# A streaming encoder step on one core: the first norm's additions and three weight splits move from GpSimd to VectorE, and the last 256 tokens of the final projection change layout

## The chip, the cores and the metric

The kernel runs on one core of one Trainium2 chip. A core has five engines that run side by side: TensorE (PE: matrix products from SBUF into the accumulation memory PSUM; the loading of its stationary operand is shown apart as PEld), VectorE (DVE), ScalarE (ACT), GpSimd (POOL) and SyncE (SP), which here only issues transfers. The metric is the device time of one execution in microseconds (us), the median over runs; lower is better. A single profiled execution supplies all durations.

## What is computed

One inference step of a two-layer encoder for 1024 frames of a new stream and 32 frames of a running one (1056 tokens, 1024 channels, fp32). The first layer has a pooling mixer, a gated MLP over chunks and a gate; the second is latent attention with a gate. Every layer normalises its input and its output:

```python
h = rms_norm(x, g_pre)                       # layer input
z = jnp.einsum('btd,de->bte', h, w_in)
...                                          # mixers, gate
y = jnp.einsum('bte,ed->btd', mix, w_out)
x = x + rms_norm(y, g_post)                  # residual
```

with `rms_norm(x, g) = x * rsqrt(mean(x*x, over channels) + 1e-6) * g`. The last lines of the second layer are `y = (o * silu(gate)) @ w_o` and `x + rms_norm(y, norm_post[1])`, where `w_o` is 1024 x 1024. The two places that matter here are the sum of squares of the very first norm and this last projection with its norm.

## The kernel before

All activations lie with channels on the 128 partitions and tokens along the free dimension, as eight blocks of 128 channels (index `k` or `m`). The tokens are cut into group a (640 tokens) and group b (416), in the last projection into 800 and 256. To keep fp32 accuracy, each operand of a product is split into two fp32r parts, hi (a rounded copy, written by ACT) and lo (the value less hi), and a product is three matmuls: hi x hi, hi x lo, lo x hi.

**Weights.** `prep_w` (L133 to L146) brings a weight block in pieces of 512 columns: SP loads a `raw` tile (three slots), ACT casts it to `whi` (L143), and an engine subtracts to get `wlo` (L144): GpSimd, unless the call passes `lo_on=nc.vector`. `whi` and `wlo` have four slots each in the common pool `stg`; calls with `pool=` get slots in a pool of their own (six each).

**Order.** TensorE's order is the order of the program text. The other engines' orders are set by a scheduling planner that simulates the kernel when it is built. Side jobs are generators: `spawn` gives one a due time in modelled TensorE nanoseconds (table `N`), and `poll`, called in the matmul loops, steps the one that is due; `drain` runs what is left. Their matmuls thereby get fixed places in TensorE's order.

**The head** (`even`, L301 to L370). Weight blocks 8 and 9 of `w1` and the eight channel blocks of x are loaded. For group a and then b, and for each `k`, `split_x` writes hi (ACT, L323) and lo (DVE, L324) of x times the pre-norm gain, TensorE multiplies with blocks 8 and 9, and `sumsq` squares x (ACT, L278 and L281) and adds the square to an accumulator (L282): on GpSimd for group a, on VectorE for group b. The norm itself is applied later, to the products: `rstd` (L193 to L233) sums the accumulator over the partitions on TensorE (L202), takes the power -1/2 on GpSimd (L210), and spreads the result over the partitions by diagonal matrices (L220), matmuls and copies (L233) into `rep`. `evac` (L185, L187) multiplies the products by `rep`, and with that frees the PSUM banks for block 10, prepared at L359, whose matmuls follow.

**The tail** (`output`, L1020 to L1098, and `final_a`, L1100 to L1118). The gated attention output comes back from DRAM by `load_og` and is split. Then the projection runs over the 800 tokens for output blocks `m` = 0 to 7, with weights `w[m]`; each result is copied (L1047), squared (L1052) and accumulated (L1053). `final_a`, spawned after that, makes the norm of these tokens and writes the output: per block a fused product on DVE (L1113), the residual addition (L1114) and a store. While it runs, TensorE does the 256 tokens, blocks 7 down to 0, where blocks 7 to 3 still lie in SBUF (3 to 5 in the six slots of pool `wx`) and 2 to 0 are loaded again. ACT squares each result and applies the gain (L1076, L1077), DVE accumulates (L1079). At the end come the column sums (L1068), the power on GpSimd (L1088), the spreading by diagonals (L1092, L1093) and, in quarters, product, residual and store (L1096 to L1098).

Of the kernel before, what the change touches and what calls it, by code (L numbers as in the profile page):

```python
# [10 lines left out]
F32 = mybir.dt.float32  # L11
F32R = mybir.dt.float32r
AF = mybir.ActivationFunctionType
ALU = mybir.AluOpType
# [5 lines left out]
P = 128  # L20
D = 1024
NK = 8
T = 1056
NA, NB, CA = 640, 416, 320
OA = 400
# [8 lines left out]

N = {"x": 462, "mix": 10626, "mixq": 1490, "tr": 717, "lead": 9945, "tr0": 11989, "res": 9194, "ra": 2699,
     "rb": 1574, "ha": 14000, "hb": 5000, "kv": 429, "q": 20908, "k": 34682, "kvs": 1773, "qs": 10662, "rest": 1357, "r1": 1608,
     "r2": 1337, "fa": 5400, "st": 6975, "w0": 2000, "w1": 1552, "f0": 1645, "f1": 626, "fy": 648}
HF = 6
RB = 4
LU = 5  # L40
NV = 1184
EPS = 1e-6
WARM = 12
# [3 lines left out]
GA1, GP1, GA2, GP2, PSC, LNG, LNB, QN, KVN = 0, 8, 16, 24, 32, 40, 48, 56, 59  # L47
# [23 lines left out]
class Build:  # L71
# [61 lines left out]
    def prep_w(self, src, n=1024, lo_on=None, pool=None):  # L133

        nc = self.nc
        res = []
        for o in range(0, n, 512):
            m = min(512, n - o)
            raw = self.t(self.stg, [P, 512], F32, "raw", bufs=3)
            hi = self.t(pool or self.stg, [P, 512], F32R, "whi", bufs=6 if pool else 4)  # L140
            lo = self.t(pool or self.stg, [P, 512], F32R, "wlo", bufs=6 if pool else 4)
            nc.sync.dma_start(raw[:, :m], src[:, o : o + m])
            nc.scalar.copy(hi[:, :m], raw[:, :m])  # L143
            (lo_on or nc.gpsimd).tensor_tensor(lo[:, :m], raw[:, :m], hi[:, :m], ALU.subtract)  # L144
            res.append((hi, lo))
        return res  # L146
# [138 lines left out]
    def even(self):  # L285
        nc = self.nc
# [9 lines left out]
        wts = {8: [], 9: []}  # L296
# [3 lines left out]
            nc.tensor.matmul(warm, self.ones, self.ones[:, None, :].to_broadcast([P, 4, P]), start=True, stop=True)  # L300
        for half in range(2):  # L301
            for i in range(2):
                wts[8 + i] += self.prep_w(self.i_w1[8 + i, :, half * 512 : half * 512 + 512], 512)
                if half == i == 0:
                    nc.sync.dma_start(xs[0][:, :NA], self.i_xT[0, :, :NA])
            for k in range(half * 4 + (half == 0), half * 4 + 4):
                nc.sync.dma_start(xs[k][:, :NA], self.i_xT[k, :, :NA])
# [4 lines left out]
        rep = self.new_rep()  # L312
# [35 lines left out]
        for g in "ab":  # L348
            acc = self.t(self.ab2, [P, NA if g == "a" else NB], F32, g)
            z = [None, None]  # L350
            for k in range(NK):
                x = split_x(g, k)
                for i in range(2):
                    z[i] = self.mm_block(self.wcol(wts[8 + i]), h, [k], g, ps=z[i], first=k == 0, last=k == 7)
                self.sumsq(acc, x, k == 0, g, nc.gpsimd if g == "a" else nc.vector, self.ab2)
            self.spawn(self.rstd(acc, g, D, rep.get(g)), N["x"])
            if g == "a":
                zz = z
        wts[10] = self.prep_w(self.i_w1[10])  # L359
        self.pos = 2  # L360
        mB[2] = self.pair(self.ab2)
        for g, z in (("a", zz), ("b", z)):
# [40 lines left out]
        for q in range(4):  # L403
            for j in range(2):
                nc.tensor.matmul(rss[:, q * 32 : (q + 1) * 32], self.ones[:32, :], wsp[q // 2][:32, q % 2, j, :32],
                                 start=j == 0, stop=j == 1)
        Cs = self.t(evc, [P, NK, 32], F32, "Cs")
        for m in range(NK):
            q = m // 2
# [163 lines left out]
        for i in range(8):  # L573
# [8 lines left out]
            if i >= 1:  # L582
                m = i - 1
# [9 lines left out]
        y = [None] * NK  # L593
        self.h2 = h2 = [None] * NK
        self.rep2 = self.new_rep()
        for g in "ab":
            n = NA if g == "a" else NB
            acc = self.t(self.V, [P, 1088], F32, "v")[:, :n] if g == "a" else self.t(self.ab2, [P, n], F32, "a")
            order = list(range(NK)) if g == "a" else list(reversed(range(NK)))
            for m, nm in zip(order, order[1:] + [None]):  # L600
# [10 lines left out]
                src = ps[0][:, :, :CA] if g == "a" else ps[1][:, :NB]  # L611
                v = two if g == "a" else (lambda z: z)
# [162 lines left out]
    def attention(self):  # L775
# [178 lines left out]
        for x, (h, i) in enumerate(steps):  # L954
# [17 lines left out]
            units(0.75)  # L972
            if h == 7 and i == LU:
                self.shut(self.carry)
                self.hl = self.open("hl", side="right", bufs=2 * HF)
                self.og = {}
            if h == 7 and i >= LU:
                for k in range(2 * (i - LU), min(HF, 2 * (i - LU + 1))):
# [41 lines left out]
    def output(self, w2, z2):  # L1020
        nc = self.nc
        na, nb = 2 * self.ca, self.nb
        hl = self.open("hlb")
        tp = self.open("tp", bufs=3)
        yp = self.open("yp", bufs=8)
        wx = self.open("wx")
        ones = self.t(tp, [P, P], F32, "ones", bufs=1)
        nc.gpsimd.memset(ones, 1.0)
        og = self.og
        w = dict(enumerate(w2))  # L1030
        for k in range(HF, 8):
            self.load_og(k, "a", hl, tp)
        for k in range(NK):
            self.load_og(k, "b", hl, tp)

        acc = self.t(tp, [P, na], F32, "acca", bufs=1)
        y = []
        for m in range(NK):
            if m in (0, 2, 3, 4, 5, 6):
                n = max(2, m + 1)  # L1040
                w[n] = self.prep_w(self.i_wo[n], pool=wx if 3 <= n < 6 else None)
            if m < 2:
                ps = self.mm_block(self.wcol(w[m]), og, range(HF, 8), "a", ps=z2[m], first=False)
            else:
                ps = self.mm_block(self.wcol(w[m]), og, range(NK), "a")
            yy = self.t(yp, [P, na], F32, "a")
            nc.vector.tensor_copy(two(yy), ps[0][:, :, : na // 2])  # L1047
            if m == 0:
                nc.scalar.activation(acc, yy, AF.Square)
            else:  # L1050
                sq = self.t(tp, [P, na], F32, "a", bufs=2)
                nc.scalar.activation(sq, yy, AF.Square)  # L1052
                nc.vector.tensor_tensor(acc, acc, sq, ALU.add)  # L1053
            y.append(yy)
        self.spawn(self.final_a(acc, y, tp, yp, na), N["fa"])


        acc = self.t(tp, [P, nb], F32, "accb", bufs=1)
        y = self.t(yp, [P, NK, nb], F32, "yb", bufs=1)
        x = self.t(yp, [P, NK, nb], F32, "xb", bufs=1)  # L1060
        nc.sync.dma_start(x, self.x1d[:, :, na:].rearrange("m p n -> p m n"))
        st = []

        def stats(src, first):
            for j in range(nb // P):
                if first:
                    st.append(self.bank("mi"))
                nc.tensor.matmul(st[j][:, 0:1], src[:, j * P : (j + 1) * P], self.one, start=first, stop=not first)  # L1068
            yield 0

        for m in reversed(range(NK)):
            if 3 <= m < 6:
                w[m - 3] = self.prep_w(self.i_wo[m - 3], lo_on=nc.vector)
            z = self.mm_block(self.wcol(w[m]), og, range(NK), "b")[1][:, :nb]
            sq = acc if m == 7 else self.t(tp, [P, nb], F32, "b")
            nc.scalar.activation(sq, z, AF.Square)  # L1076
            nc.scalar.activation(y[:, m], z, AF.Copy, scale=self.vec(GP2, m))  # L1077
            if 0 < m < 7:
                nc.vector.tensor_tensor(acc, acc, sq, ALU.add)  # L1079
            if m == 1:  # L1080
                self.spawn(stats(acc, True), N["st"])
        self.drain()
        for _ in stats(sq, False):
            pass
        ms = self.t(self.cst, [P, 8], F32, "sm", bufs=4)[:, : nb // P]
        for j in range(nb // P):
            nc.vector.tensor_scalar(ms[:, j : j + 1], st[j][:, 0:1], 1.0 / D, EPS, ALU.mult, ALU.add)
        nc.gpsimd.tensor_tensor(ms, ms, self.mhalf[:, : nb // P], ALU.pow)  # L1088
        rep = self.bank("za")[:, 0, :nb]
        for j in range(nb // P):  # L1090
            dg = self.t(tp, [P, P], F32, "dg", bufs=2)
            nc.vector.tensor_scalar(dg, self.ident, ms[:, j : j + 1], None, ALU.mult)  # L1092
            nc.tensor.matmul(rep[:, j * P : (j + 1) * P], ones, dg, start=True, stop=True)  # L1093
        for q in range(4):
            v = slice(2 * q, 2 * q + 2)
            nc.vector.tensor_tensor(y[:, v], y[:, v], rep[:, None, :].to_broadcast([P, 2, nb]), ALU.mult)  # L1096
            nc.vector.tensor_tensor(y[:, v], y[:, v], x[:, v], ALU.add)
            (nc.sync if q % 2 else nc.scalar).dma_start(self.o_yT[v, :, na:].rearrange("m p n -> p m n"), y[:, v])  # L1098

    def final_a(self, acc, y, tp, yp, n):  # L1100
        nc = self.nc
# [38 lines left out]
def pack(x_prompt, x_sample, cache_pool, cache_ckv, cache_krope, norm_pre, norm_post, w_in_even, w_pool, pool_scale,  # L1140
         sgu_ln_g, sgu_ln_b, w_spatial, b_spatial, w_out_even, w_in_odd, q_norm, kv_norm, w_q_up, w_kv_up, w_o):
    c = np.ascontiguousarray
    a = {}
# [26 lines left out]
    a["wo"] = c(w_o[0].reshape(NK, P, NK, P).transpose(2, 1, 0, 3).reshape(NK, P, 1024))  # L1170
    cc = cache_ckv[0, 0].T.reshape(2, P, P).transpose(1, 0, 2)
    ck = np.concatenate([cache_krope[0, 0].T] * 2, 0)[:, None]
    a["cache"] = c(np.concatenate([cc, ck], 1))
    pos = np.concatenate([np.arange(1024), 128 + np.arange(32)]).astype(np.float32)
    freqs = np.float32(10000.0) ** (-np.arange(32, dtype=np.float32) / np.float32(32))
# [5 lines left out]
    return a  # L1181


OUTS = {"yT": (NK, P, T), "st": (P, NK, 30), "sv": (32, D), "ckvT": (2, P, T), "krT": (64, T)}


@with_exitstack
# [26 lines left out]
```

## Time and profile before

| | us |
|---|---|
| median of 3 runs | 1336.59 (1332.97 to 1336.67) |
| the profiled execution | 1338.32 |
| its span, first to last instruction | 1336.5 |
| busy in the span: PE, DVE, ACT, POOL | 1297.6, 706.2, 491.2, 406.1 |
| mean granted TensorE clock | 0.986 |

The profile's times count from the start of the span. A row in order of time gives start, duration, engine, line of the kernel, operation, output and inputs, shape and count, and in brackets how long the engine had been idle and what released it. A group's row gives busy time and mean duration in ns, then idle time and its releasers. A row by stretch gives the stretch, its length, the busy time and instruction count of PE, PEld, DVE, ACT and POOL, the granted clock, the share of the DMA engines that is busy, and GB/s.

### The profile page before, as it was taken

Reading aid. Unit: us, or ns where it says so; the run is one execution under the profiler, and the core shown is the slowest. Engines: PE = TensorE matmul, PEld = TensorE weight load, DVE = VectorE, ACT = ScalarE, POOL = GpSimd, SP = SyncE. Lnnn points to the kernel's source line nnn. Section 1 sums busy time; section 2 is a strip of 40 time slices with the busy share of each in tenths; the row PEclk is TensorE's granted clock in tenths of the full one; section 3 lists DMA queues with packets and bytes.
Section 4 is the critical chain, followed back from the end, with each engine's and each line's share of the span. In section 5 each row is a group of like instructions: output and inputs, shape, how many; then the busy total and the mean of one; then the engine's idle time right before and its main releaser. Section 6 shows DMA issues by size and latency. Waiting matters only on the chain.

```text
span 1336.5 us, 21136 instructions
## 1 busy us (share of the span) xinstructions
PE 1297.6 (97%) x8244; PEld 1269.4 (95%) x8244; DVE 706.2 (53%) x1359; ACT 491.2 (37%) x968; POOL 406.1 (30%) x452
## 2 busy tenths in 40 slices
PE   8899999999999999999999989999999999999995
PEld 7899999999999999999999989999999999998994
DVE  7412021976956443533286642743666666665337
ACT  6212122222123333422154322434556565645221
POOL 6322112577743222200001354322223322323200
PEclk9899999999999999999999989999999999999997
DMA  5111111111111111222266333322111111126305
GB/s 191 48 48 56 48 40 48 40 40 33 52 43 45 52 48 40 70 73 78 63 215 194 109 111 102 119 83 65 46 49 46 47 46 51 47 65 219 97 25 179
DMA packets 63155, 102.62 MB, mean 77 GB/s; under 512 B 9232, under 2 KB 28080, under 8 KB 63056
## 3 DMA queue, kind: packets, MB, share of 16 engines
q1 hardware_dynamic: 51168, 86.17, 21.3%
q10 hardware_dynamic: 11888, 15.11, 3.2%
q8 instruction: 65, 1.06, 0.3%
q14 instruction: 34, 0.28, 0.1%
HBM read 82.34 MB, written 18.91 MB: 76 GB/s over the span
## 4 chain that ended last, share of the span: by engine, by line
PE 84%; DVE 7%; issue 3%; ACT 1%; DMA 1%; POOL 1%; ACTq 0%; DVEq 0%; POOLq 0%
PE za L108 36%; PE zb L108 21%; PE pj L108 12%; PE sc L108 11%; PE pj L905 2%; PE mi L108 1%; DMA raw<-in_wout 1%; PE mi L202 1%; PE mi L423 1%; ACT sw L829 0%; DVE b L324 0%; DVE b L637 0%; DVE b L659 0%; DVE v L536 0%; DVE b L648 0%
## 5 line engine op out<-in xcount | busy, mean ns | idle before, releaser
L108 PE MATMUL za<-a,whi 128*128 128x320 f32 x2112 | 463.6, 314 | 1.9 <-ACT a L323 1.2
L108 PEld LDWEIGHTS za<-a,whi 128*128 128x128 f32 x2112 | 371.8, 189 | 5.2 <-ACT a L323 1.6
L144 POOL TENSOR_TENSOR wlo<-raw,whi 128x512 fp32r<-128x512 f32 (+2 forms) x168 | 223.1, 1331 | 418.8 <-ACT whi L143 398.9
L108 PE MATMUL zb<-b,whi 128*128 128x416 f32 x1024 | 339.1, 356 | 1.5 <-DVE b L187 1.5
L143 ACT CAST whi<-raw 128x512 fp32r<-128x512 f32 (+2 forms) x230 | 139.3, 607 | 515.9 <-PE zb L108 260.8
L108 PE MATMUL za<-a,wlo 128*128 128x320 f32 x1056 | 242.0, 311 | 1.9 <-POOL wlo L144 1.8
L108 PEld LDWEIGHTS zb<-b,whi 128*128 128x128 f32 x1024 | 194.0, 191 | 2.5 <-DVE b L187 1.6
L108 PEld LDWEIGHTS za<-a,wlo 128*128 128x128 f32 x1056 | 192.1, 189 | 3.0 <-POOL wlo L144 2.5
L108 PE MATMUL zb<-b,wlo 128*128 128x416 f32 x512 | 181.2, 354 | 0.7 <-DVE wlo L144 0.7
L185 DVE TENSOR_TENSOR a<-za,repa 128x640 f32<-128x640 f32 x38 | 31.1, 821 | 162.9 <-PE za L108 162.8
L878 POOL TENSOR_SCALAR p<-p,nm 128x128 f32<-128x128 f32 (+8 forms) x72 | 53.0, 736 | 164.3 <-DVE nm L877 129.0
L108 PEld LDWEIGHTS zb<-b,wlo 128*128 128x128 f32 x512 | 98.1, 192 | 1.6 <-DVE wlo L144 1.0
L210 POOL TENSOR_TENSOR sm<-sm,mhalf 32x1 f32<-32x1 f32 (+3 forms) x17 | 15.3, 906 | 237.9 <-DVE sm L209 237.9
L144 DVE TENSOR_TENSOR wlo<-raw,whi 128x512 fp32r<-128x512 f32 x62 | 42.3, 688 | 56.8 <-ACT whi L143 56.8
L876 ACT ACTIVATE p<-sc,nm 128x128 f32<-128x128 f32 (+8 forms) x72 | 50.6, 703 | 44.7 <-DVE nm L875 33.3
L108 PE MATMUL sc<-a,whi 128*128 128x400 f32 x256 | 57.7, 346 | 0.7 <-DVE a L1047 0.4
L908 DVE TENSOR_TENSOR pl<-pj,ph 128x512 fp32r<-128x512 f32 (+2 forms) x96 | 51.1, 552 | 7.0 <-ACT ph L907 6.3
L875 DVE TENSOR_REDUCE nm<-sc 128x1 f32<-128x128 f32 (+8 forms) x72 | 50.7, 704 | 3.2
L907 ACT CAST ph<-pj 128x512 fp32r<-128x512 f32 (+2 forms) x96 | 43.8, 481 | 20.4 <-PE pj L905 18.1
L108 PEld LDWEIGHTS sc<-a,whi 128*128 128x128 f32 x256 | 46.3, 188 | 1.6 <-DVE a L1047 0.7
L108 PE MATMUL pj<-pl,vh 128*128 128x256 f32 (+1 forms) x160 | 45.1, 282 | 0.2 <-DVE pl L908 0.2
L108 PE MATMUL pj<-ph,vl 128*128 128x256 f32 (+1 forms) x160 | 45.0, 281 | 0.0
(292 smaller groups left out, 2300.7 us busy)
## 6 DMA issues: line engine op xcount, KB each, us to landing
raw<-in_w SPq DMA_DIRECT2D x120, 256.0 KB, 2.7
raw<-in_wout SPq DMA_DIRECT2D x60, 256.0 KB, 3.1
raw<-in_wo SPq DMA_DIRECT2D x22, 256.0 KB, 3.1
gt<-gated SPq DMA_DIRECT2D x32, 128.0 KB, 2.5
ogd<-og ACTq DMA_DIRECT2D x32, 128.0 KB, 2.6
v<-in_xT SPq DMA_DIRECT2D x16, 208.0 KB, 4.5
rawa<-x1d SPq DMA_DIRECT2D x8, 400.0 KB, 3.9
out_yT<-a SPq DMA_DIRECT2D x8, 400.0 KB, 4.6
```

The lines of the kernel that those rows point to most:

```text
L108: self.nc.tensor.matmul(out, lhsT, rhs, start=start, stop=stop)
L143: nc.scalar.copy(hi[:, :m], raw[:, :m])
L144: (lo_on or nc.gpsimd).tensor_tensor(lo[:, :m], raw[:, :m], hi[:, :m], ALU.subtract)
L185: nc.vector.tensor_tensor(two(dst.a), ps[0][:, :, :CA], two(rep.a), ALU.mult)
L202: nc.tensor.matmul(st[:w, j : j + 1], acc[:, j * P : j * P + w], self.one, start=True, stop=True)
L210: nc.gpsimd.tensor_tensor(m[:w, c0:c1], m[:w, c0:c1], self.mhalf[:w, c0:c1], ALU.pow)
L875: nc.vector.tensor_reduce(nm[:n, 0:1], view, axis=AX.XY, op=ALU.max, negate=True)
L876: nc.scalar.activation(pv, view, AF.Exp, bias=nm[:n, 0:1], accum_out=nm[:n, 1:2])
L878: nc.gpsimd.tensor_scalar(p[:n, :K], p[:n, :K], nm[:n, 2:3], 1.0, ALU.mult, ALU.mult)
L905: nc.tensor.transpose(tr[:, e, :], p[:, (b + e) * P : (b + e + 1) * P], self.ident)
L907: nc.scalar.copy(hi[:, :nb, off : off + P], tr[:, :nb, :])
L908: nc.vector.tensor_tensor(lo[:, :nb, off : off + P], tr[:, :nb, :], hi[:, :nb, off : off + P], ALU.subtract)
```

## The change

At the head, group a's additions of squares (L282) go to VectorE, as group b's did, and so do the `wlo` subtractions of blocks 8, 9 and 10 of `w1`.

At the tail, the last 256 tokens are computed with tokens on the partitions: two tiles of 128 tokens by 1024 channels in PSUM. The split tokens are the stationary operand and `w_o`, now by contraction block `k` (a new input, `wok`), the moving one, 512 columns at a time. Blocks 0 and 1 are prepared during the 800 tokens (GpSimd subtracts), 2 and 3 at their end, 4 to 7 four steps ahead (VectorE subtracts). Up to `k` = 4 the two tiles alternate; then the first is finished, and then the second. x is turned to token layout by 16 transposes in the side job `turn`. Since a token's channels now lie along the free dimension, ACT's square with accumulation gives its sum directly, and no sums over partitions or spreading are left; the gain is a loaded broadcast (`gb`). The output of these tokens is stored in token layout. The pool `wx` changes from six slots to four, and blocks 3 to 5 of the 800 tokens' weights now use the common slots.

```diff
-                wts[8 + i] += self.prep_w(self.i_w1[8 + i, :, half * 512 : half * 512 + 512], 512)
+                wts[8 + i] += self.prep_w(self.i_w1[8 + i, :, half * 512 : half * 512 + 512], 512, lo_on=nc.vector)
...
-                self.sumsq(acc, x, k == 0, g, nc.gpsimd if g == "a" else nc.vector, self.ab2)
+                self.sumsq(acc, x, k == 0, g, nc.vector, self.ab2)
...
-        wts[10] = self.prep_w(self.i_w1[10])
+        wts[10] = self.prep_w(self.i_w1[10], lo_on=nc.vector)
...
-                w[n] = self.prep_w(self.i_wo[n], pool=wx if 3 <= n < 6 else None)
+                w[n] = self.prep_w(self.i_wo[n])
+            if m in (3, 5):
+                wr[m // 2 - 1] = self.prep_w(self.i_wok[m // 2 - 1], pool=wx)
+            if m == 7:
+                for k in (2, 3):
+                    wr[k] = self.prep_w(self.i_wok[k], lo_on=nc.vector)
...
+        gb = self.t(yp, [P, D], F32, "gb", bufs=1)
+        nc.sync.dma_start(gb, self.i_gp2bc)
+        xt = [self.t(yp, [P, D], F32, "xt", bufs=nt) for _ in range(nt)]
+        def turn():
+            for j in range(nt):
+                for c in range(2):
+                    pt = self.bank("mi")
+                    for q in range(4):
+                        nc.tensor.transpose(pt[:, q * P : (q + 1) * P], x[:, c * 4 + q, j * P : (j + 1) * P], self.ident)
+                        self.now += 107
+                    nc.scalar.copy(xt[j][:, c * 512 : (c + 1) * 512], pt)
+                    yield N["tn"]
+        self.spawn(turn(), N["tn"])
+        z = [self.bank("za") for _ in range(nt)]
+        def tile_k(j, k):
+            xh, xl = (v.b[:, j * P : (j + 1) * P] for v in og[k])
+            for c in range(2):
+                hi, lo = wr[k][c]
+                for e, (xx, w) in enumerate(((xh, hi), (xh, lo), (xl, hi))):
+                    self.mm(z[j][:, c, :], xx, w, k == 0 and e == 0, k == NK - 1 and e == 2, 512)
+                self.poll()
+        for k in range(KS):
+            for j in range(nt):
+                tile_k(j, k)
+            if k + 4 < NK:
+                wr[k + 4] = self.prep_w(self.i_wok[k + 4], lo_on=nc.vector, pool=wx if k < 2 else None)
+        for j in range(nt):
+            for k in range(KS, NK):
+                tile_k(j, k)
+            if j == 0:
+                self.drain()
+            yg = self.t(yp, [P, D], F32, "yg", bufs=nt)
+            st = self.t(self.cst, [P, 8], F32, "sm", bufs=4)
+            for c in range(2):
+                junk = self.t(tp, [P, na], F32, "a", bufs=2)
+                nc.scalar.activation(junk[:, :512], z[j][:, c, :], AF.Square, accum_out=st[:, c : c + 1])
+            nc.vector.tensor_tensor(yg.rearrange("p (c n) -> p c n", c=2), z[j],
+                                    gb.rearrange("p (c n) -> p c n", c=2), ALU.mult)
+            nc.vector.tensor_tensor(st[:, 2:3], st[:, 0:1], st[:, 1:2], ALU.add)
+            nc.vector.tensor_scalar(st[:, 3:4], st[:, 2:3], 1.0 / D, EPS, ALU.mult, ALU.add)
+            nc.gpsimd.tensor_tensor(st[:, 4:5], st[:, 3:4], self.mhalf[:, 0:1], ALU.pow)
+            for c in range(2):
+                v = slice(c * 512, (c + 1) * 512)
+                nc.vector.scalar_tensor_tensor(yg[:, v], yg[:, v], st[:, 4:5], xt[j][:, v], ALU.mult, ALU.add)
+                (nc.sync if c else nc.scalar).dma_start(self.o_yL[j * P : (j + 1) * P, v], yg[:, v])
```

`KS` is 5 and `N["tn"]` 1800. What the new loop replaces (L1071 to L1098) is in the listing above.

More of the change, by code (lines that the diff above doesn't have):

```diff
@@ L36 @@
      "rb": 1574, "ha": 14000, "hb": 5000, "kv": 429, "q": 20908, "k": 34682, "kvs": 1773, "qs": 10662, "rest": 1357, "r1": 1608,
-     "r2": 1337, "fa": 5400, "st": 6975, "w0": 2000, "w1": 1552, "f0": 1645, "f1": 626, "fy": 648}
+     "r2": 1337, "fa": 5400, "tn": 1800, "w0": 2000, "w1": 1552, "f0": 1645, "f1": 626, "fy": 648}
 HF = 6
@@ L40 @@
 LU = 5
+KS = 5
 NV = 1184
@@ L139, in prep_w @@
             raw = self.t(self.stg, [P, 512], F32, "raw", bufs=3)
-            hi = self.t(pool or self.stg, [P, 512], F32R, "whi", bufs=6 if pool else 4)
-            lo = self.t(pool or self.stg, [P, 512], F32R, "wlo", bufs=6 if pool else 4)
+            hi = self.t(pool or self.stg, [P, 512], F32R, "whi", bufs=4)
+            lo = self.t(pool or self.stg, [P, 512], F32R, "wlo", bufs=4)
             nc.sync.dma_start(raw[:, :m], src[:, o : o + m])
@@ L1026, in output @@
         wx = self.open("wx")
-        ones = self.t(tp, [P, P], F32, "ones", bufs=1)
-        nc.gpsimd.memset(ones, 1.0)
         og = self.og
+        wr = {}
         w = dict(enumerate(w2))
@@ L1055, in output @@
         self.spawn(self.final_a(acc, y, tp, yp, na), N["fa"])
-        acc = self.t(tp, [P, nb], F32, "accb", bufs=1)
-        y = self.t(yp, [P, NK, nb], F32, "yb", bufs=1)
+        nt = nb // P
         x = self.t(yp, [P, NK, nb], F32, "xb", bufs=1)
         nc.sync.dma_start(x, self.x1d[:, :, na:].rearrange("m p n -> p m n"))
[L1062 to L1098, printed above, removed]
+        gb = self.t(yp, [P, D], F32, "gb", bufs=1)
+        nc.sync.dma_start(gb, self.i_gp2bc)
+        xt = [self.t(yp, [P, D], F32, "xt", bufs=nt) for _ in range(nt)]
@@ L1172, in pack @@
     ck = np.concatenate([cache_krope[0, 0].T] * 2, 0)[:, None]
+    a["wok"] = c(w_o[0].reshape(NK, P, D))
+    a["gp2bc"] = c(np.broadcast_to(norm_post[1][None], (P, D)))
     a["cache"] = c(np.concatenate([cc, ck], 1))
@@ L1181, in pack @@
     return a
-OUTS = {"yT": (NK, P, T), "st": (P, NK, 30), "sv": (32, D), "ckvT": (2, P, T), "krT": (64, T)}
+OUTS = {"yT": (NK, P, 2 * OA), "yL": (T - 2 * OA, D), "st": (P, NK, 30), "sv": (32, D), "ckvT": (2, P, T), "krT": (64, T)}
 @with_exitstack
@@ L1206 @@
     c = np.ascontiguousarray
-    y = np.asarray(r["out_yT"]).reshape(D, T).T
+    y = np.concatenate([np.asarray(r["out_yT"]).reshape(D, 2 * OA).T, np.asarray(r["out_yL"])], 0)
     st = np.asarray(r["out_st"]).transpose(1, 0, 2).reshape(D, 30).T
```

## Prediction, on record before the changed kernel ran

> **What bounds the kernel now.** I read the busy time by stretch first, then the instructions in order of time at both ends, then the groups by line, and the chain of waits only for two durations.
>
> ```profile
> 5.00:26.00 21.00, 17.09 (x102) 14.79 (x100) 17.94 (x11) 20.63 (x36) 18.76 (x11) 1.00 0.74 271
> 26.00:44.00 18.00, 14.26 (x62) 13.15 (x63) 14.44 (x28) 2.53 (x5) 7.26 (x7) 0.81 0.10 30
> ```
> ```profile
> 935.00:1195.00 260.00, 259.00 (x1813) 248.06 (x1812) 172.28 (x427) 153.82 (x373) 76.36 (x95) 1.00 0.17 48
> ```
> ```profile
> 1290.00:1306.00 16.00, 15.41 (x119) 14.36 (x118) 9.33 (x26) 5.28 (x11) 2.44 (x6) 1.00 0.16 50
> 1306.00:1318.00 12.00, 11.69 (x98) 11.49 (x96) 11.96 (x16) 4.36 (x11) 0.00 (x0) 1.00 0.70 210
> 1318.00:1337.00 19.00, 3.09 (x12) 2.71 (x12) 11.40 (x20) 0.53 (x2) 0.70 (x1) 0.60 0.48 182
> ```
>
> Columns: stretch, length, busy PE, PEld, DVE, ACT, POOL, clock, DMA. In the middle TensorE is never short of work (259.00 of 260), so what is saved at the head arrives at the end. Room is at the two ends, the parts edited. Between 26 and 44 TensorE works 14.26 of 18, at a clock of 0.81; after 1318 it works 3.09 of 19. The head in order of time:
>
> ```profile
> 6.85 0.92 DVE L324 SCALAR_TENSOR_TENSOR a<-v,vecs,a 128x640 fp32r<-128x640 f32 x1 [5.76 <-ACT a L323]
> 10.17 11.95 DVE L324 SCALAR_TENSOR_TENSOR a<-v,vecs,a 128x640 fp32r<-128x640 f32 x6 [0.16 <-ACT a L323]
> 19.28 8.02 POOL L282 TENSOR_TENSOR a<-a,a 128x640 f32<-128x640 f32 x4
> 22.05 3.86 DVE L324 SCALAR_TENSOR_TENSOR b<-v,vecs,b 128x416 fp32r<-128x416 f32 x2
> 25.83 1.92 DVE L282 TENSOR_TENSOR b<-b,b 128x416 f32<-128x416 f32 x1
> 27.35 1.48 PE L202 MATMUL mi<-one,a 128*128 128x1 f32 x10 [1.58 <-POOL a L282]
> 27.67 0.64 DVE L324 SCALAR_TENSOR_TENSOR b<-v,vecs,b 128x416 fp32r<-128x416 f32 x1
> 28.23 0.58 DVE L282 TENSOR_TENSOR b<-b,b 128x416 f32<-128x416 f32 x1
> 32.34 0.52 DVE L220 TENSOR_SCALAR dgh<-ident,rh 128x128 fp32r<-128x128 f32 x2 [1.33 <-POOL rh L211]
> 34.30 3.80 POOL L144 TENSOR_TENSOR wlo<-raw,whi 128x512 fp32r<-128x512 f32 x2 [1.71 <-PE zb L108]
> 35.31 1.67 DVE L324 SCALAR_TENSOR_TENSOR b<-v,vecs,b 128x416 fp32r<-128x416 f32 x1
> 36.91 1.47 DVE L220 TENSOR_SCALAR dgh<-ident,rh 128x128 fp32r<-128x128 f32 x2
> 42.52 0.29 DVE L233 COPY repa<-mi 128x128 f32<-128x128 f32 x1 [2.19 <-PE mi L108]
> 43.82 0.82 PE L108 MATMUL za<-a,whi 128*128 128x320 f32 x4 [0.15 <-DVE a L185]
> ```
>
> The reader is to see one thing: a DVE operation takes 0.92 (640 columns) or 0.64 (416) when POOL is still, and 1.99 (11.95/6) or 1.93 (3.86/2) while POOL adds or subtracts. POOL's four adds from 19.28 end at 27.30, exactly where DVE falls back to 0.64 and where TensorE's L202 starts. POOL does not relieve DVE; it doubles it, and DVE carries the chain from 22 to 43.
>
> **The change at the head.** Seven adds (L282) and six subtractions (L144: four for w1's blocks 8 and 9, two for block 10) leave POOL for DVE. Their price on DVE is in the groups of later stages, beside the product's:
>
> ```profile
> L144 DVE TENSOR_TENSOR wlo<-raw,whi 128x512 fp32r<-128x512 f32 x56 | 38.3, 689 | 56.2 <-ACT whi L143 56.2
> L648 DVE SCALAR_TENSOR_TENSOR a<-a,vecs,a 128x640 fp32r<-128x640 f32 x8 | 7.0, 880 | 0.0
> L282 DVE TENSOR_TENSOR v<-v,a 128x640 f32<-128x640 f32 x7 | 5.8, 826 | 2.4 <-ACT a L281 2.4
> ```
>
> DVE operations back to back start some 0.07 before the one ahead ends (27.67 to 28.23 is 0.56 for a 0.64), so I count 0.81, 0.76 and 0.62 for the three forms. Group a, from the second product at 8.82: seven products 5.7, seven adds 5.3, two subtractions 1.2 (two more fall into DVE's early gaps): 12.2 with 0.4 for the odd wait is 12.6, against 13.2 now (8.82 to 22.05): -0.6. Group b: two products -2.7 (3.86 less 1.2), one add -1.3, the product at 35.31 -1.0, the pair of L220 at 36.91 -0.95 (the same pair takes 0.52 at 32.34), together -6.0; block 10's two subtractions +1.4 (2 x 0.689): -4.6. ACT, full until then (20.63 of 21), hands over group a's last square at 18.5, so it does not hold DVE back. TensorE is no floor there: the sums' L202 find group a's accumulator complete at about 21.5 instead of 27.3, and its 47 remaining products of group b at 0.185 need 8.7, less than DVE's run. Block 10's weights, now on DVE behind the products, are cast as soon as TensorE lets go of the slots of block 8 and are due only after the run, so 1.4 is their whole price; behind them wait L220 and L185, already in the sum. The head gives -5.2. From both sides: if only half of DVE's stretching (7.1 in group a, 14.1 less 7.0, and 6.0 in group b) goes with POOL, it is 7.9 of new work less 6.5, +1.4; if also DVE's idle 1.33 before 32.34 and the slow clock at 39.2 (below, 1.2) go, -7.7.
>
> **The change at the tail.** The last 256 tokens: 192 matmuls of 256 columns with the weight stationary become 96 of 512 with the tokens stationary; 16 transposes of x1, a load of the broadcast gain (512 KB) and eight contraction blocks of w_o in place of three reloaded output blocks (ten more loads of 256 KB) come in; the column sums, the broadcast of the norm, ACT's 16 passes over the blocks and DVE's six adds and eight output operations go out. Rows of the chain of waits (transposes; matmuls of 512 columns), of the order of time and of the groups:
>
> ```profile
> 1198.36 0.44 PE pj L905 x4
> ```
> ```profile
> 1208.08 2.33 PE sc L108 x10
> ```
> ```profile
> 1306.16 1.05 DVE L1113 SCALAR_TENSOR_TENSOR a<-a,vecs,repa 128x800 f32<-128x800 f32 x1
> 1317.05 0.28 PE L108 MATMUL pj<-b,wlo 128*128 128x256 f32 x1
> 1317.41 0.28 PE L108 MATMUL pj<-b,wlo 128*128 128x256 f32 x1
> 1321.49 1.89 DVE L1114 TENSOR_TENSOR a<-a,rawa 128x800 f32<-128x800 f32 x2
> 1325.25 0.16 DVE L1087 TENSOR_SCALAR sm<-pj 128x1 f32<-128x1 f32 x1 [1.53 <-PE pj L1068]
> 1325.92 0.70 POOL L1088 TENSOR_TENSOR sm<-sm,mhalf 128x2 f32<-128x2 f32 x1 [25.55 <-DVE sm L1087]
> 1331.92 1.29 DVE L1097 TENSOR_TENSOR yb<-yb,xb 128x512 f32<-128x512 f32 x2
> ```
> ```profile
> L143 ACT CAST whi<-raw 128x512 fp32r<-128x512 f32 x6 | 3.7, 617 | 1.8 <-PE pj L108 1.4 <-issue 0.3
> L1096 DVE TENSOR_TENSOR yb<-yb,sc 128x512 f32<-128x512 f32 x4 | 2.6, 682 | 1.2 <-PE sc L1093 1.2
> L1079 DVE TENSOR_TENSOR accb<-accb,b 128x256 f32<-128x256 f32 x6 | 2.5, 418 | 0.6 <-ACT b L1076 0.6
> ```
>
> TensorE gains nothing: three 256-column matmuls take 0.36 (1317.05 to 1317.41), so 192 take 23.0; 96 at 0.233 take 22.4; the transposes (two steps of the chain view's 0.44 for four, so 1.8 for 16) bring its end from 1317.7 to about 1318.9. The gain is in what follows. Were DVE free, the last tile would need a square, the power and two outputs, about 4, and the 3.3 that lie now between DVE's last end (1333.2) and the span's (1336.5): 1326. But DVE is full from 1306 on (11.96 of 12). From 1306.15, where the group of 800 tokens gets its norm: that group's 16 operations, now from 1306.16 to 1323.4 with three of L1079's adds (0.35 each after overlap) and two subtractions (0.62) among them: 17.2 less 2.3 is 14.9; the last weight block's two subtractions 1.2; per 128-token tile a product out of PSUM over 1024 (two of L1096, 1.36), two small ones (0.16 each) and two fused outputs over 512 (0.74, between 0.64 at 416 and 0.88 at 640): 3.2, two tiles 6.3, less overlap 5.8. DVE ends at 1328.0, plus half of one power's wait (0 to 1.0) 1328.5, plus the first transposes ahead of the 800 tokens' sums 0.4, plus 3.3: 1332.2. The tail gives -4.3. From both sides: no wait and no delay -5.2; DVE left standing for late weights, below, -1.8, and I hold 0 possible.
>
> Edits at nothing, with the row that covers them:
>
> ```profile
> 1237.00:1290.00 53.00, 52.58 (x290) 52.47 (x290) 15.67 (x19) 11.25 (x18) 7.46 (x6) 1.00 0.19 56
> ```
>
> W_o blocks 3 to 5 lose their own six slots, so each waits for the block two ahead; its casts and subtractions (2 x 0.617 on ACT, on POOL 3.80 at worst, by 34.30) have a block of 8.8 as cover (the 800 tokens' last six blocks fill the 53.00 of the row, POOL being busy 7.46 of it); uncovered they would cost 5.0 a block. On ACT behind that cast stand the squares, for which only the accumulator waits. ACT gets ten more casts, four copies and four squares of some 0.62 and loses 16 passes, and is busy 5.28 of 16 and 4.36 of 12. SP's added loads go where DMA is a sixth busy (0.16 above), behind nothing that is due before 1290. The subtractions of blocks k = 2 to 6 fall before 1306, where DVE is busy 9.33 of 16.
>
> GpSimd's power is the one operation left beside a full DVE. [...]
>
> **Sum.** -5.2 - 4.3 = -9.5. The profiled execution took 1338.32 (span 1336.5, 1.82 around it) and would take 1328.8; the median of the runs lies 1.73 lower, so 1336.59 - 9.5 = **1327.1**.
>
> **Rivals.** (1) Late weights: block 7 of w_o is free to be cast only after k = 3, about 1305, and its subtractions may stand on DVE behind the 800 tokens' 16 operations. TensorE then waits until 1306.15 + 14.9 + 1.2 = 1322.3, runs 24 matmuls (5.6), then square, power and outputs (3.5) and 3.3: 1334.7, tail -1.8, 1336.6 - 7.0 = 1329.6. For it: DVE's order is fixed by a planner; against: these precede in the program.
> (2) Clock. TensorE's idle spells at the head are followed by slow stretches:
>
> ```profile
> 39.20 0.90 PE L108 MATMUL zb<-b,whi 128*128 128x416 f32 x2
> 42.94 0.54 PE L108 MATMUL zb<-b,whi 128*128 128x416 f32 x2
> 54.29 0.65 PE L108 MATMUL zb<-b,whi 128*128 128x416 f32 x2 [1.55 <-DVE b L187]
> 55.53 0.84 PE L108 MATMUL zb<-b,whi 128*128 128x416 f32 x2
> ```
>
> Fewer idle spells could spare the ones at 39.2 (nine products, 1.2) and from 55.5 (about 1.7): 1327.1 - 2.9 = 1324.2. Against: the 1.55 of idling before 54.29 stays. [...]
> (3) The other side: DVE's long durations belong to the stage, not to POOL. Then the moved work is stretched too: seven adds at 1.92 and the two subtractions at 3.80 make 17.2 on DVE's chain, less 4.3: 1349.5. It decides as soon as less than a quarter of the 13.1 of stretching goes (7.9 - 13.1f = +4.3, f = 0.27). Against it: 0.64 and 1.93 for one form, three operations apart.
> (4) Head as summed but half, tail nothing, because the planner's order leaves DVE standing for POOL or PSUM: -2.6, 1334.0.
>
> **Chances.** Forecast 0.52, (1) 0.15, (2) 0.18, (3) 0.04, (4) 0.11. A measurement of this kernel tells about 0.3% (4.0) from no change. The first three cases are faster; (4) is the same: faster 0.85, same 0.10, slower 0.05. Range: (2) with the better bounds, 1320.5, to past (1), 1333.
>
> **What would show it.** Right: DVE's 640-column product at about 0.9 throughout; L202 at about 23 to 24; the first L108 on block 10 near 38.6; TensorE's end near the old 1318.9 less the head's gain, with DVE still busy some 9 longer. Wrong: products still near 1.9; a TensorE wait for wlo in the last 30; a stretch after TensorE's end in which DVE is idle.

## The result

The changed kernel takes 1325.74 us (median of five runs, 1324.0 to 1329.64) against 1336.38 for the kernel before (five runs, 1332.97 to 1336.67): a ratio of 0.993, 95% interval 0.9908 to 0.9953, so 10.6 less by the medians, and between 6.3 and 12.3 by the interval. The forecast was 1327.1. Lines of the changed kernel up to L900 are one higher than before (L325 is the product that was L324).

### The profile after

The busy time by stretch of the changed kernel (stretch, length, busy PE, PEld, DVE, ACT, POOL, clock, DMA share, GB/s):

```profile
5.00:26.00 21.00, 19.93 (x125) 18.47 (x124) 17.80 (x27) 19.62 (x34) 1.70 (x3) 1.00 0.72 267
26.00:44.00 18.00, 16.13 (x100) 14.97 (x99) 13.32 (x35) 6.21 (x9) 5.07 (x9) 1.00 0.19 60
44.00:61.00 17.00, 15.45 (x93) 15.19 (x92) 3.00 (x5) 4.26 (x7) 3.87 (x3) 1.00 0.14 47
1290.00:1306.00 16.00, 14.82 (x67) 11.65 (x68) 14.18 (x29) 4.23 (x9) 0.42 (x3) 1.00 0.29 94
1306.00:1318.00 12.00, 2.17 (x10) 1.48 (x8) 11.55 (x17) 1.27 (x4) 1.06 (x2) 0.76 0.78 310
```

One row of the same view of the kernel before that was not shown yet:

```profile
44.00:61.00 17.00, 15.45 (x90) 15.05 (x90) 5.04 (x16) 5.75 (x9) 5.41 (x9) 0.90 0.13 38
```

In the first stretch POOL falls from 18.76 to 1.70 and DVE stays at 17.8 (17.94 before), though it does 27 instructions there where it did 11. The granted clock between 26 and 61, 0.81 and 0.90 before, is 1.00. From 1306 on TensorE is nearly done while DVE is full.

The product's group in the first 32 us of the kernel before:

```profile
L324 DVE SCALAR_TENSOR_TENSOR a<-v,vecs,a 128x640 fp32r<-128x640 f32 x8 | 14.1, 1806 | 7.0 <-ACT a L323 7.0
```

The same group of the changed kernel, then its DVE in order of time, then TensorE:

```profile
L325 DVE SCALAR_TENSOR_TENSOR a<-v,vecs,a 128x640 fp32r<-128x640 f32 x8 | 7.0, 880 | 0.6 <-ACT a L324 0.6
```
```profile
8.48 0.89 DVE L325 SCALAR_TENSOR_TENSOR a<-v,vecs,a 128x640 fp32r<-128x640 f32 x1 [0.21 <-ACT a L324]
...
17.35 0.88 DVE L325 SCALAR_TENSOR_TENSOR a<-v,vecs,a 128x640 fp32r<-128x640 f32 x1
18.14 0.82 DVE L283 TENSOR_TENSOR a<-a,a 128x640 f32<-128x640 f32 x1
18.88 0.88 DVE L325 SCALAR_TENSOR_TENSOR a<-v,vecs,a 128x640 fp32r<-128x640 f32 x1
...
20.41 0.65 DVE L325 SCALAR_TENSOR_TENSOR b<-v,vecs,b 128x416 fp32r<-128x416 f32 x1
...
25.85 0.52 DVE L221 TENSOR_SCALAR dgh<-ident,rh 128x128 fp32r<-128x128 f32 x2 [1.34 <-POOL rh L212]
...
33.28 0.28 DVE L234 COPY repa<-mi 128x128 f32<-128x128 f32 x1
33.48 1.28 DVE L145 TENSOR_TENSOR wlo<-raw,whi 128x512 fp32r<-128x512 f32 x2
34.68 1.54 DVE L186 TENSOR_TENSOR a<-za,repa 128x640 f32<-128x640 f32 x2
```
```profile
22.63 1.17 PE L203 MATMUL mi<-one,a 128*128 128x1 f32 x10
...
35.55 0.86 PE L109 MATMUL za<-a,whi 128*128 128x320 f32 x4 [1.43 <-DVE a L186]
```

The product over 640 columns takes 0.88 throughout (a mean of 1.806 before), the added squares 0.82 each, and DVE turns to group b at 20.41 instead of 22.05. Block 10 starts at 35.55 instead of 43.82.

The end, on DVE, POOL and TensorE, in order of time:

```profile
1287.43 0.67 DVE L145 TENSOR_TENSOR wlo<-raw,whi 128x512 fp32r<-128x512 f32 x1
1290.01 0.53 DVE L221 TENSOR_SCALAR dgh<-ident,rh 128x128 fp32r<-128x128 f32 x2 [1.91 <-POOL rh L212]
...
1291.48 0.47 DVE L221 TENSOR_SCALAR dgl<-ident,sm 128x128 fp32r<-128x128 f32 x2
...
1295.42 0.23 DVE L221 TENSOR_SCALAR dgl<-ident,sm 32x32 fp32r<-32x32 f32 x1 [0.18 <-PE pj L109]
1296.75 0.69 DVE L145 TENSOR_TENSOR wlo<-raw,whi 128x512 fp32r<-128x512 f32 x1 [1.10 <-ACT whi L144]
1297.36 0.45 DVE L234 COPY repa<-pj 128x288 f32<-128x288 f32 x1
1297.73 0.68 DVE L145 TENSOR_TENSOR wlo<-raw,whi 128x512 fp32r<-128x512 f32 x1
1298.33 2.01 DVE L1129 SCALAR_TENSOR_TENSOR a<-a,vecs,repa 128x800 f32<-128x800 f32 x2
...
1313.25 1.22 DVE L1106 TENSOR_TENSOR yg<-sc,gb 128x1024 f32<-128x1024 f32 x1
...
1316.39 2.74 DVE L1113 SCALAR_TENSOR_TENSOR yg<-yg,sm,xt 128x512 f32<-128x512 f32 x4 [0.41 <-POOL sm L1110]
```
```profile
1287.53 2.30 POOL L211 TENSOR_TENSOR sm<-sm,mhalf 128x6 f32<-128x6 f32 x2 [23.83 <-DVE sm L210]
```
```profile
1279.29 0.39 PE L109 MATMUL sc<-whi,b 128*128 128x512 f32 x1
...
1293.04 0.28 PE L109 MATMUL pj<-dgh,ones 128*128 128x256 f32 x1
...
1294.63 0.35 PE L109 MATMUL pj<-dgh,ones 128*128 128x256 f32 x1 [0.50 <-DVE dgh L221]
...
1296.64 0.28 PE L109 MATMUL pj<-dgh,ones 32*128 32x32 f32 x1
...
1307.79 0.39 PE L109 MATMUL sc<-whi,b 128*128 128x512 f32 x1
```

And of the kernel before, for the same points (the start of the 256 tokens; the power; the first diagonal):

```profile
1289.99 0.39 PE L108 MATMUL pj<-b,whi 128*128 128x256 f32 x2
```
```profile
1297.93 1.85 POOL L210 TENSOR_TENSOR sm<-sm,mhalf 128x6 f32<-128x6 f32 x2 [48.78 <-DVE sm L209]
```
```profile
1299.97 0.53 DVE L220 TENSOR_SCALAR dgh<-ident,rh 128x128 fp32r<-128x128 f32 x2 [2.07 <-POOL rh L211]
```

TensorE starts the 256 tokens at 1279.29 and ends at 1308.2, 28.9 later. DVE runs on to 1319.1, and the span ends at 1322.2: 42.9 from the start of the 256 tokens, where it was 46.5 (1336.5 less 1289.99).

So the span of the profiled execution falls by 14.3: 10.7 by the start of the 256 tokens and 3.6 behind it. Of the 10.7, 8.3 are there at block 10. Between 44 and 61 the clock of 0.90 is gone: 17.00 x 0.10 is 1.7 us of full speed. The 0.7 left lies in the long middle. The two profiled executions lie at opposite sides of their medians (1338.32 against 1336.38, and 1324.03 against 1325.74), which takes 14.3 to the 10.6 of the medians.

### The profile page after: what moved, and what is told of

It reads as the page before. It is cut to its first block, busy times and chain, and to the rows that moved or that the text cites. A ratio compares the mean times of both kernels' runs of the same rounds, so it can differ in the third digit from the quotient of the medians.

```text
span 1322.2 us, 20987 instructions
## 1 busy us (share of the span) xinstructions
PE 1289.3 (98%) x8152; PEld 1257.9 (95%) x8152; DVE 703.0 (53%) x1370; ACT 496.3 (38%) x974; POOL 389.0 (29%) x443
## 4 chain that ended last, share of the span: by engine, by line
PE 85%; DVE 8%; issue 2%; DMA 1%; POOL 1%; ACT 1%; SPq 0%; ACTq 0%; DVEq 0%; POOLq 0%
PE za L109 36%; PE zb L109 20%; PE sc L109 12%; PE pj L109 11%; PE pj L906 2%; PE mi L109 1%; DMA raw<-in_wout 1%; PE mi L203 1%; PE mi L424 1%; DVE a L1129 1%; ACT sw L830 1%; DVE wlo L145 1%; DVE b L660 0%; DVE b L638 0%; DVE b L649 0%
## 5 line engine op out<-in xcount | busy, mean ns | idle before, releaser
L144 ACT CAST whi<-raw 128x512 fp32r<-128x512 f32 (+2 forms) x240 | 145.5, 608 | 538.0 <-PE zb L109 255.0
L145 POOL TENSOR_TENSOR wlo<-raw,whi 128x512 fp32r<-128x512 f32 (+2 forms) x166 | 219.1, 1321 | 429.6 <-ACT whi L144 417.2
L145 DVE TENSOR_TENSOR wlo<-raw,whi 128x512 fp32r<-128x512 f32 x74 | 50.6, 688 | 68.4 <-ACT whi L144 68.2
L908 ACT CAST ph<-pj 128x512 fp32r<-128x512 f32 (+2 forms) x96 | 43.8, 480 | 20.5 <-PE pj L906 18.1
```

The lines of the kernel that those rows point to most:

```text
L908: nc.scalar.copy(hi[:, :nb, off : off + P], tr[:, :nb, :])
```

## The experiments

The theory: DVE is slowed by GpSimd's operations that read SBUF; the head's gain is that, and the tail's end is set by DVE's own work. The rivals: the long durations belong to the stage or to any activity of GpSimd; the two halves depend on each other; the tail is held by weights or by GpSimd's power. Each kernel ran beside the kernel before on the same chip: the first four on one, where the kernel before takes 1335.86 (29 runs), the other four on a second, where it takes 1335.41 (13 runs).

### Each half alone

The kernel before with the head's three edits:

```diff
+ wts[8 + i] += self.prep_w(..., 512, lo_on=nc.vector)
+ self.sumsq(acc, x, k == 0, g, nc.vector, self.ab2)
+ wts[10] = self.prep_w(self.i_w1[10], lo_on=nc.vector)
```

> The kernel before with the head's edits alone (adds of group a and the subtractions of w1's blocks 8 to 10 on VectorE). Sharing theory (VectorE operations double only while GpSimd reads SBUF): all 640-column products at 0.88, TensorE's first matmul on block 10 at 35.6 instead of 43.8, the time 7 to 11 below before, the spread coming from slow-clock windows. Rival (the forecast's own sum, -5.2): block 10 at 38.6, 5 below. The tail, from TensorE's start on the 256 tokens to the span's end, stays at 46.5.

And the changed kernel with these three undone:

```diff
- wts[8 + i] += self.prep_w(..., 512, lo_on=nc.vector)
+ wts[8 + i] += self.prep_w(..., 512)
- self.sumsq(acc, x, k == 0, g, nc.vector, self.ab2)
+ self.sumsq(acc, x, k == 0, g, nc.gpsimd if g == "a" else nc.vector, self.ab2)
- wts[10] = self.prep_w(self.i_w1[10], lo_on=nc.vector)
+ wts[10] = self.prep_w(self.i_w1[10])
```

> The changed kernel with its head put back as before (adds and subtractions on GpSimd). If the two ends are independent: block 10 again at 43.8, the tail 42.9 long instead of 46.5, the time 3 to 5 below before, and the two single edits together give the whole change. Rival (what was gained at the head depends on the tail's new order of loads, or the reverse): the two do not add up to the whole by more than 2.

The head alone: 1329.93, ratio 0.996 (0.9946 to 0.9974), 5.9 less. The tail alone: 1332.21, ratio 0.9974 (0.9964 to 0.9984), 3.65 less. Their sum, 9.6, is the whole within the intervals, so neither half needs the other. In the traces the head alone keeps the old tail (46.5 from the start of the 256 tokens to the end), and the tail alone has the new one (43.0). The head alone starts block 10 at 35.59, as the theory had it (35.6), but its time is not 7 to 11 less: 5.9 lies near the 5 of the forecast's own sum. DVE in order of time with the old head, in the kernel with the tail alone:

```profile
32.22 0.52 DVE L221 TENSOR_SCALAR dgh<-ident,rh 128x128 fp32r<-128x128 f32 x2 [1.34 <-POOL rh L212]
...
41.08 0.29 DVE L234 COPY repa<-mi 128x128 f32<-128x128 f32 x1 [0.86 <-PE mi L109]
```

And TensorE in order of time in that kernel:

```profile
39.01 0.54 PE L109 MATMUL zb<-b,whi 128*128 128x416 f32 x2
```

This is the same head as before, with TensorE's slow stretch elsewhere (its products at 39 take 0.54 for two, where the kernel before had 0.90), and its block 10 starts at 42.38, where 43.8 was expected. DVE's wait for the last spread of the norm is 0.86 here, where it was 2.19 in the kernel before at 42.52. So 1.33 of that wait goes with the clock. The rest of it has no counterpart in the row at 33.28 of the changed kernel.

### Each part of the head alone

The additions moved, the subtractions left on GpSimd; and the other way round (both against the kernel before):

```diff
- self.sumsq(acc, x, k == 0, g, nc.gpsimd if g == "a" else nc.vector, self.ab2)
+ self.sumsq(acc, x, k == 0, g, nc.vector, self.ab2)
```

> The kernel before with only the seven adds of group a moved. Sharing theory: GpSimd then reads only during six subtractions, so only the products beside those are stretched (four of eight in group a, about one each); block 10's first matmul at about 38 to 39, the time 4 to 7 below before. Rival (what counted was TensorE's wait for GpSimd's accumulator, 1.6 at 27.35): the time about 2 below.

```diff
- wts[8 + i] += self.prep_w(..., 512)
+ wts[8 + i] += self.prep_w(..., 512, lo_on=nc.vector)
- wts[10] = self.prep_w(self.i_w1[10])
+ wts[10] = self.prep_w(self.i_w1[10], lo_on=nc.vector)
```

> The kernel before with only the six subtractions of w1's blocks 8 to 10 moved. Sharing theory: GpSimd's seven adds keep the products beside them at 1.9, and VectorE has four more operations in group a, so group a ends no earlier; only block 10's part is relieved (about 2): the time 0 to 3 below before. Rival (what counted was TensorE's wait for GpSimd's wlo, 1.8 at 19.37, and block 10's late weights): 4 or more below.

The additions alone give 1332.56, ratio 0.9979 (0.9971 to 0.9988), 3.3 less; the subtractions alone 1334.01, ratio 0.9989 (0.998 to 0.9998), 1.85 less, which is barely clear of no change. The additions fall short of the 4 to 7 expected: block 10 starts at 40.19, not at 38 to 39. Its two subtractions, still on GpSimd from 29.24 on, stretch a product and an addition of DVE to 1.68 and 1.64, and a slow stretch of TensorE falls there too (clock 0.81 from 26 to 44), so that DVE waits 2.56 for the last spread. With the additions moved, POOL and DVE in order of time:

```profile
10.77 1.45 POOL L144 TENSOR_TENSOR wlo<-raw,whi 128x512 fp32r<-128x512 f32 x1 [1.92 <-ACT whi L143]
12.65 1.40 POOL L144 TENSOR_TENSOR wlo<-raw,whi 128x512 fp32r<-128x512 f32 x1 [0.42 <-ACT whi L143]
```
```profile
10.98 1.92 DVE L282 TENSOR_TENSOR a<-a,a 128x640 f32<-128x640 f32 x1
12.83 1.91 DVE L324 SCALAR_TENSOR_TENSOR a<-v,vecs,a 128x640 fp32r<-128x640 f32 x1
14.66 0.81 DVE L282 TENSOR_TENSOR a<-a,a 128x640 f32<-128x640 f32 x1
```

Where these two subtractions run, the two DVE operations beside them take 1.9, and the next one takes 0.81. With the subtractions moved it is POOL's additions that stretch DVE, its subtractions too, until they end:

```profile
9.18 14.00 POOL L282 TENSOR_TENSOR a<-a,a 128x640 f32<-128x640 f32 x7 [8.31 <-ACT a L281]
```
```profile
11.43 2.05 DVE L144 TENSOR_TENSOR wlo<-raw,whi 128x512 fp32r<-128x512 f32 x1
...
24.59 1.20 DVE L324 SCALAR_TENSOR_TENSOR b<-v,vecs,b 128x416 fp32r<-128x416 f32 x2
```

The time is within the 0 to 3 expected. In the trace block 10 starts at 40.16, 3.7 earlier than in the kernel before, and 2.2 earlier than in the old head whose slow stretch lay elsewhere (42.38, above). The reason stands in these rows: POOL, rid of four subtractions, ends its additions at 23.2 instead of 27.3, and from 24.59 on group b's two products take 1.20 where they took 3.86.

### GpSimd's reading or its being busy

The changed kernel, with GpSimd made to add each of group a's squares to itself into a tile that is not in use there; then with two memsets of that tile in place of each of GpSimd's additions:

```diff
  eng.tensor_tensor(acc, acc, sq, ALU.add)
+ if dup is not None:      # given for group a
+     dup(sq)
...
+ scr = rep.a
+ def dup(sq):
+     nc.gpsimd.tensor_tensor(scr, sq, sq, ALU.add)
```

> The changed kernel with seven needless GpSimd adds of 640 columns put beside group a (they read the squares and write a tile that is overwritten later; no result depends on them). Sharing theory: VectorE's 640-column products and adds go back to about 1.9 while they run, VectorE's group a ends some 8 to 14 later, block 10's first matmul at 42 to 47 instead of 35.6, the time 6 to 11 above the changed kernel's. Rival (VectorE's long durations belonged to the stage, its loads and its ScalarE work): 0.88 stays, block 10 at 35.6 to 36, no change of the time.

```diff
+ def dup(sq):
+     for _ in range(2):
+         nc.gpsimd.memset(scr, 0.0)
```

> The same, but GpSimd writes the tile with two memsets beside each square instead of adding: busy at the same places, reading nothing. If it is GpSimd's reading that doubles VectorE: 0.88 stays, block 10 at about 35.6, the time that of the changed kernel within 2. If any GpSimd work does: as with the adds, in proportion to how long the memsets last.

With reads: 1334.53, ratio 0.9997 (0.9984 to 1.001); the whole gain is lost, and block 10 starts at 46.30. POOL and DVE in order of time:

```profile
9.90 3.11 POOL L353 TENSOR_TENSOR repa<-a 128x640 f32<-128x640 f32 x2 [9.05 <-ACT a L282]
13.70 8.75 POOL L353 TENSOR_TENSOR repa<-a 128x640 f32<-128x640 f32 x5 [0.68 <-ACT a L282]
```
```profile
11.83 1.87 DVE L327 SCALAR_TENSOR_TENSOR a<-v,vecs,a 128x640 fp32r<-128x640 f32 x1
13.62 0.81 DVE L283 TENSOR_TENSOR a<-a,a 128x640 f32<-128x640 f32 x1
...
21.27 1.87 DVE L327 SCALAR_TENSOR_TENSOR a<-v,vecs,a 128x640 fp32r<-128x640 f32 x1
...
23.79 0.87 DVE L327 SCALAR_TENSOR_TENSOR a<-v,vecs,a 128x640 fp32r<-128x640 f32 x1
```

The operation that DVE starts in POOL's pause from 13.0 to 13.7 takes 0.81 after 1.87; then the durations rise again, and they fall for good when POOL's last addition ends at 22.45. Nothing on DVE's side differs between these rows. With memsets the time is 1325.74, ratio 0.9925 (0.9909 to 0.9942), that of the changed kernel itself. POOL and DVE in order of time:

```profile
0.79 9.59 POOL L354 MEMSET repa<- 128x640 f32 x14
```
```profile
8.75 0.88 DVE L327 SCALAR_TENSOR_TENSOR a<-v,vecs,a 128x640 fp32r<-128x640 f32 x1
9.55 0.82 DVE L283 TENSOR_TENSOR a<-a,a 128x640 f32<-128x640 f32 x1
```

The memsets did not stand beside each square, as the expectation had it. They read no square, so nothing held them back, and all 14 were done at 10.38, where the additions of the run before went on to 22.45. The time of this run therefore does not separate reading from being busy. Its rows do, for the few operations that stand beside memsets: DVE's two products at 6.88 and 8.75 take 0.88, the addition at 9.55 takes 0.82, and two subtractions 0.69, all as when POOL is still. So, as far as these five show it, it is what GpSimd reads, not that it works, that doubles DVE's operations: one product takes 1.87 beside the additions and 0.88 beside the memsets. DVE's diagonals, made from one tile and a column of scalars, are slowed too: two take 1.72 at 39.24 in the changed kernel, where POOL subtracts from 39.59 to 40.87, and 0.52 at 25.85.

### The tail: when the norm arrives, and who sets the end

The changed kernel with earlier due times for the norm of the 800 tokens; and the changed kernel without the 800 tokens' residual additions:

```diff
- "fa": 5400, ... "f1": 626
+ "fa": 2400, ... "f1": 300
```

> The changed kernel with two due times shortened: the sums of the 800 tokens' norm 2400 instead of 5400 after their last matmul, and 300 instead of 626 between the pieces of its spreading. Theory (after TensorE's last stage VectorE alone sets the end, from the moment the norm of the 800 tokens arrives): its first L1129 some 3 to 4 earlier relative to the start of the 256 tokens (19.0 now), and the tail 39 to 40 instead of 42.9: 3 to 4 below the changed kernel. Rival (TensorE then waits for the power on GpSimd, and the epilogue becomes late): the tail gains 1 at most.

```diff
- nc.vector.tensor_tensor(y[m], y[m], xr[m], ALU.add)
```

> The changed kernel without the eight residual additions of the 800 tokens (L1130; the loads of x stay): their output lacks the residual. They are about 7.4 of VectorE's work after the norm arrives. If VectorE is the bound: its end 6 to 7 earlier, until TensorE's end (1308) and the last tile's epilogue are next, the tail 36 to 37 instead of 42.9. Rival (the stores of 3.3 MB, DMA 0.78 busy in the last stretch, are the bound already): 2 or less.

Earlier norm: 1323.12, ratio 0.9906 (0.9891 to 0.9921), 2.6 less than the changed kernel's 1325.74. The kernel with the memsets, which took 1325.74 on the same chip, has its fastest run at 1325.42 and this one its slowest at 1323.74. It beats both kernels. DVE in order of time:

```profile
1295.36 1.05 DVE L1129 SCALAR_TENSOR_TENSOR a<-a,vecs,repa 128x800 f32<-128x800 f32 x1
...
1301.56 1.29 DVE L145 TENSOR_TENSOR wlo<-raw,whi 128x512 fp32r<-128x512 f32 x2
```

The norm is there 14.05 after the start of the 256 tokens (1281.31 in this trace) instead of 19.04, and the tail is 39.8 instead of 42.9. Three weight subtractions now stand between the 800 tokens' operations (two of them at 1301.56), at some 0.6 each, so of the 5.0 by which the norm is earlier 3.1 reach the end. Without the residual additions: 1319.62, ratio 0.9879 (0.9865 to 0.9894), 6.1 less than the changed kernel; its tail is 36.9. Eight additions at 0.94 are 7.5; some 6 of it came through, because the last epilogue is then no longer packed against the other one and waits 0.67 and 0.66 for the two powers. TensorE's products were the same in all three, and ended 28.9, 28.0 and 28.9 after the start of the 256 tokens. So DVE's work after the norm's arrival sets the end, as the working had it, and the earlier arrival was worth about 3.

## Why the prediction was right

**The time** (1327.1 forecast, 1325.74 measured) and the signs of both parts were right; each part was off by 0.7, the head to the better side and the tail to the worse.

**Head: -5.2 forecast, -5.9 alone.** The mechanism held: the product at 0.88 throughout, spacing 0.79 and 0.74 in the rows from 17.35 to 18.88 (0.81 and 0.76 taken), block 10's two subtractions 1.28 (1.4 taken). The rival by which the long durations belong to the stage is refuted by the same rows, and by the additions put back. Group a was forecast from 13.2 to 12.6; it took 11.93 (8.48 to 20.41), because no odd wait came and the operations followed a little closer than taken, and it began 0.34 earlier: -1.6 in place of -0.6. Group b was forecast at -4.6. It took 15.14 to block 10 (20.41 to 35.55), against 21.77 before (22.05 to 43.82): -6.6. The step that failed is the list of what was removed there: it did not count DVE's wait of 2.19 at 42.52 for TensorE's last spread of the norm, which went as well. It had instead named the idle 1.33 before the diagonals as what might go, and that one stayed (1.34 at 25.85). "TensorE is no floor there" was not quite so either: DVE now waits 0.65 for the sums of L203. The waits together explain 1.5 of the 2.0 that were missed; the rest lies in the operations. By the tail-alone kernel, 1.33 of the 2.19 goes with the clock, which varies from execution to execution (a mean of 0.986 to 0.99 over the 29 runs of the kernel before). That is one reason why the profiles differ by 8.3 at block 10 and the timed runs by only about 6; where the rest stays is open, since the head-alone kernel too has block 10 at 35.59. L202's sums came at 22.63 (23 to 24 forecast) and block 10 at 35.55 (38.6 forecast).

**Tail: -4.3 forecast, -3.65 alone.** TensorE's part was exact: 28.9 from the start to the end of its work. The 800 tokens' operations took 14.92 (1298.33 to 1313.25; 14.9 forecast), the epilogues 5.9 with the power's wait (1313.25 to 1319.13; 5.8 and 0.5), and 3.1 remained to the end of the span (3.3). The mis-sized term is the norm's arrival: 0.4 later by the working, 19.0 after the start of the 256 tokens instead of 16.2 by the trace, 2.9 later. 0.75 of it stood already at the first diagonal (10.72 against 9.98), 0.45 of that in the power itself, 2.30 for two instead of 1.85, with a DVE subtraction running beside it. The other 2.1 lies between the first diagonal and the first L1129: 8.32 here (1290.01 to 1298.33), 6.19 before (1299.97 to 1306.16). Most of it is TensorE's order, for which the sum had only the 0.4 of the transposes. The second group of diagonals is complete at 1291.95 and its product runs at 1293.04; the last one is complete at 1295.65 and its product runs at 1296.64. In both gaps, 1.1 and 1.0, TensorE is at its other products without a pause; before, the corresponding two gaps were none and 0.3. The step "the subtractions of blocks 2 to 6 fall before 1306, where DVE is busy 9.33 of 16" put at nothing the subtractions that now stand in DVE's order there. The ones at 1296.75 and 1297.73 hold up the last copy by 0.3 and the first L1129 by 0.6; but the kernel before had a subtraction and an addition in that place too, so this is at most a small part of the difference. With the earlier due times three subtractions stand among the diagonals and the stretch takes 6.41. The last weight block's 1.2, which I had placed behind the norm, fell ahead of it, and so part of the loss came back. The tail's nearness to the forecast is in part luck: 2.5 more than forecast for the arrival, less this 1.2, 0.4 in the epilogues and 0.2 at the end. That earlier due times shorten the tail by 3.1 shows the arrival as the cause; the subtractions alone were not moved.

**The rivals.** Late weights did not come: TensorE has no wait behind 1294.63, and it ends as forecast. The clock did move as the second rival had it, in the profile: the slow stretches between 26 and 61 are gone, 5.1 us of lost full speed before (18.00 x 0.19 and 17.00 x 0.10). But the head-alone kernel has a clock of 0.90 between 44 and 61 again, and the tail-alone kernel 0.81 between 26 and 44, so the change does not abolish them. It may make them fewer: the mean clock is 0.9887 over the six runs of the head alone and 0.9875 over the 29 of the kernel before, with the same tail. That would be an estimated 1.6 us of full speed (0.0012 of 1330), a part of the 5.9 that no run here separates. The lower end of the range does not follow from the working: 1324.2 less the idle 1.33 and the 0.9 of the tail's better bound is 1322.0, not 1320.5. "Half head, no tail" is refuted by the two halves run alone.

**GpSimd's power.** The sum had 0.5 for it, half a wait of a DVE operation; no run shows that term. The two powers of the epilogues took 0.55 each (1315.80 to 1316.86 together), the first beside small operations of DVE alone, and DVE's wait was 0.41. The pair over 128x6 took 0.45 longer beside a DVE subtraction (2.30 and 1.85, above).

## What to carry to other kernels

An engine that looks relieved can be the one that is slowed: compare one operation's duration where the other engine works and where it is still (1.99 and 0.92 here), before counting instructions; here seven additions moved onto the engine that carried the chain, and it finished sooner. A side job has fixed places in TensorE's order, so when the products around it change, compare when its inputs are ready with when it runs; here two of its products stood 1.1 and 1.0 behind their inputs. Work that is free by the busy share of its engine can still delay what stands behind it in that engine's order (0.6 at 1297.73), so ask of each added instruction what is due next on that engine. If the end is set by an engine's queue behind one arrival, bring the arrival forward: two due times gave 2.6.

## What the runs showed of the hardware

- Memsets on GpSimd, beside five of VectorE's operations on two tiles, cost them nothing (0.88, 0.82 and 0.69, as alone), where an addition into the same tile brought the product to 1.87.
- It is not always VectorE that loses: at 34.10 in the changed kernel GpSimd's subtraction takes 1.79, where one with VectorE idle takes 1.29 (at 49.18), while VectorE's pair at 33.48 keeps its 1.28.
- TensorE's clock goes with the scatter between runs of one kernel. Of the 29 runs of the kernel before, the seven at a mean clock of 0.986 have a median of 1337.49 and the four at 0.989 one of 1333.74; 0.003 of 1335 is 4.0, of a difference of 3.75. In the head the lost clock comes in like amounts: the clock of the kernel before is 0.50 from 38.5 to 41.8 and from 55.6 to 58.9, and 1.00 from 41.9 to 55.4; at half speed, 0.81 over 18.00 is 6.8 us and 0.90 over 17.00 is 3.4. The slow stretches lie at 28.2 to 31.6, 38.4 to 41.8 and 55.5 to 58.9 in that trace, each 3.4 long at a clock of 0.51 or 0.52, so two and one of them give the 6.8 and 3.4. They begin 10.2 and 17.1 apart, three and five times 3.4. That is one trace; that others keep to such a spacing was not shown.
- GpSimd's two powers over 128x6 took 2.30 with a VectorE subtraction beside them and 1.85 without.
